# Layer 1's products with the high and low part of h side by side: 512 + 256 columns in place of three times 256

## The chip, the core and the metric

The kernel runs on one of the eight cores of one Trainium2 chip. The metric is device microseconds of one execution. Below, TensorE (PE; its weight loads are shown as PEld), VectorE (DVE), ScalarE (ACT), GpSimd (POOL) and SyncE (SP) are the engines of the core. SBUF is the working memory of 128 partitions, PSUM the accumulators into which TensorE writes. Each engine runs its own instructions in order and waits on semaphores of the others.

## The reference, cut to what matters

Two layers work on a latent stream x (256 tokens) and a context stream ctx (256 tokens), both of width 2048. Each layer makes h from a stream (RMS norm, then a scale and a shift that come from `c` or `c_ctx` through `w_mod`), multiplies it by `w_in` (2048 x 5120), sends the columns through three kinds of branches, each with its own gate, and multiplies the joined result by `w_out`:

```python
h = rmsnorm(x, g_pre[l]) * (1.0 + scale[:, None]) + shift[:, None]
proj = h @ w_in[l]                      # and proj_c = h_c @ w_in[l] for the context
a_u, a_v, a_g, b_q, b_k, b_v, b_g, c_x, c_g = split_cols(proj)
y_a = chunk_gmlp(gelu(a_u), gelu(a_v), ...) * silu(a_g)
y_b = window_attention(rope(b_q), rope(b_k), b_v, k_ctx, v_ctx, sink) * silu(b_g)
y_c = fourier_mix(c_x, w_f, b_f) * silu(c_g)
y = rmsnorm(concat(y_a, y_b, y_c) @ w_out[l], g_post[l])
x = x + gate[:, None] * y
```

In the last layer (layer 1) the context is used for keys and values only: every other column of `proj` is needed for the 256 latent tokens alone. All is float32; the kernel has to come close to that.

## The kernel before, in words

**Precise products from parts.** A float32 operand is split into a part `hi` that the fast matmul format (fp32r) holds exactly, and the rest `lo`. A product is three matmuls, hi·hi, hi·lo and lo·hi, into the same PSUM tile (`mm3`, lines 384 to 386). Weights come by DMA as 128x1024 halves of a unit into `raw`; ScalarE casts them to `whi` (L367), VectorE subtracts to get `wlo` (L368). `Stream` fetches three halves ahead; `raw` has three buffers, `whi` and `wlo` four each.

**Where h lies.** For each of the 16 k tiles of 128 features there are two SBUF tiles of 512 columns: `hh[k]` has the high part of the 256 latent tokens and then of the 256 context tokens, `hl[k]` the low parts in the same places. `make_h` fills them: VectorE multiplies (L451), ScalarE adds the shift and casts (L455), VectorE subtracts (L458).

**Units.** Most of `w_in` is worked off in units of 128 columns: `tunit` holds a 128x128 piece of the weights still in TensorE and sends h through it, 16 k tiles, three matmuls each, into one PSUM tile. In layer 0 h is 512 columns wide (both streams). In layer 1 it is 256 (latents), but for the two k units, which need both streams. a_v, v and the output projection of layer 1 are the other way around: h stands still and the weights move. Layer 1 begins with a_v and two heads of a_u, k tile by k tile (`start_av`, `start_au`), and goes on with au (2 units), cx (4), ag (4), cg (4), k (2), v, q (8), bg (8).

**Who takes a unit's product.** a_u: a gelu on ScalarE. c_x: `fourier`, with copies on ScalarE and sums on VectorE (L624), and further products. Gates: `gate`, a tanh on ScalarE (L735) and two VectorE steps (L736, L737). q and k: `rope`, four rotation copies of 32 partitions on ScalarE (L650), products with cosine and sine on VectorE (L652 to L654), then a split into hi and lo (L401, L402). All of them read the product where it lies, in PSUM.

**Attention of a head.** After the rope come the scores (`ps_sc`), the max on VectorE (L674), the exponential on ScalarE (L694), the scaling (L702), the transposition on TensorE (`ps_tp`, L722), a split of the result (L401, L402) and the products with v (`ps_o`).

**The order of the work.** TensorE's order is written out by hand: `Later` hands steps of the branches to TensorE after a given amount of product work, counted in `tick`. On the other engines a scheduler orders the instructions by priority when the kernel is built, so what is added moves other work too; the order is then fixed. VectorE also works off, behind all that, the products for layer 1's gate from `w_mod` (L245, L247), whose loads (`mraw`) share SP's queue with those of the weights. While layer 1's first units run, the context's stream is finished: its sums (`ps_rs`), its reciprocal rms as a diagonal (L412, L414 on POOL, L421) and the broadcast of that by a product (`ps_rb`, L433).

**Buffers.** Short-lived tiles share seven buffers of 2 KB per partition (`w2k`). Six PSUM banks (`mm`) serve the products, two (`ms`) the small ones.

Of the kernel before, what the change touches and what calls it, by code (L numbers as in the profile page):

```python
# [13 lines left out]
P = 128  # L14
# [13 lines left out]
def units():  # L28
    """(name, first column, columns, first k tile, k tiles): blocks of w_in of 128 x 2048 each."""
# [37 lines left out]
def trunk_kernel(ctx: ExitStack, tc: tile.TileContext, xT, xhalf, cT, wss, wsl, wmod, win, wout0, wout1, const, vec, rows,  # L67
# [24 lines left out]
    # ---- constants  # L92
# [17 lines left out]
    class low:  # L110
        """instructions that may wait for the next `n`."""
# [22 lines left out]
    # ---- modulation: columns [128, 16, stream] of scale, shift and gate  # L134
# [5 lines left out]
    def mod_cols(l, cb, ps8):  # L140
        """ps8 [128, 4, 2]: silu(c) @ w_mod for 512 columns of column block cb."""
# [12 lines left out]
    def mod_start(k0, nk):  # L154
        """scale and shift of k tiles k0 .. k0 + nk - 1 of layer 0 on the tensor engine: yields after
        each unit's products, and before the columns."""
# [39 lines left out]
    def mod_dve(l, cb, red):  # L196
        """red [128, 2, 16]: sums over the 32 partitions of each quadrant, transposed."""
# [38 lines left out]
    def mod_gate1():  # L236
        """products of silu(c) and the gate's columns of w_mod in layer 1, still to be summed over partitions."""
# [16 lines left out]
    def gate1():  # L254
        """(sum + b_mod) * g_post of layer 1's gate, on all partitions."""
# [31 lines left out]
    def pace():  # L287
        """steps of the modulation due per half of a unit, behind the latest weights on the vector engine."""
        state["owed"] += RATE.get(state["phase"], 0.0) / 2
        while state["owed"] >= 1:  # L290
            state["owed"] -= 1
            with low(LAG), tc.issue_after(W.last.ins):
                next(mods, None)

    # ---- work of other engines that hands products back to the tensor engine later
# [32 lines left out]
    # ---- weights: raw -> exact parts hi + lo, in halves of a unit, ahead of their use  # L328
# [59 lines left out]
    def part(w, c):  # L388
        """columns c of both parts; a part is a tile or a list of tiles side by side."""
# [19 lines left out]
    # ---- per-token reciprocal rms from sums over features  # L409
# [14 lines left out]
    def col_sums(ps, q, n, start=True, stop=True):  # L424
        """columns of ps: sums over the partitions of q [128, n * 128], one accumulation group."""
# [10 lines left out]
    # ---- streams in feature-major tiles  # L436
# [7 lines left out]

    def make_h(l, k, rb, streams):
        """h = x * rstd * gs + sh, as hi + lo; rb: rstd over the tokens of `streams`."""
# [6 lines left out]
        for s in streams:  # L453
            sl = slice(s * S, (s + 1) * S)
            first = A.activation(hh[k][:, sl], t[:, sl], AF.Identity, bias=sh[l][:, k, s:s + 1])  # L455
        for s in streams:
            sl = slice(s * S, (s + 1) * S)
            last = V.scalar_tensor_tensor(out=hl[k][:, sl], in0=t[:, sl], scalar=sh[l][:, k, s:s + 1],  # L458
                                          in1=hh[k][:, sl].bitcast(F32), op0=ALU.add, op1=ALU.subtract)
# [13 lines left out]
    def tunit(n, sl=None):  # L473
        """feature-major product of one unit of 128 columns: PSUM [128, n]."""
# [8 lines left out]
        return ps  # L483

# [10 lines left out]
    # ---- one layer, up to the inputs of the output projection  # L495
    def layer(l):
# [12 lines left out]
        # a_v (token-major) and two heads of a_u, k outermost  # L509
        av = [mm_ps("av") for _ in range(nt)]  # L510
        au = [mm_ps("au") for _ in range(2)]
        def start_av(k, ts):
            c = slice((k % 2) * 512, (k % 2 + 1) * 512)
            for t in ts:
                sl = slice(t * P, (t + 1) * P)
                mm3(av[t], (hh[k][:, sl], hl[k][:, sl]), part(avw, c), k == 0, k == KT - 1)

        def start_au(k):
            for j in range(2):
                c = slice((k % 4) * 256 + j * P, (k % 4) * 256 + (j + 1) * P)  # L520
                mm3(au[j][:, 0:n], part(auw, c), (hh[k][:, 0:n], hl[k][:, 0:n]), k == 0, k == KT - 1)
# [57 lines left out]
        # branch A  # L579
        def branch_a():  # L580
            vt = [w2k([P, 512]) for _ in range(nt)]
            ss = sb([P, 4], F32, "ss")
            for j in range(2):
                A.activation(ytmp(j), au[j][:, 0:n], AF.Gelu_apprx_tanh)
# [20 lines left out]
        # branch C  # L605
# [9 lines left out]
        def fourier(g, ps):  # L615
            """cos(2 pi t m / 256) is even in t around 128 and sin odd: positions t and 256 - t are added for the one
# [478 lines left out]
```

## Time and profile before

| what | value |
|---|---|
| median of 3 runs | 1171.56 us (1171.32 to 1173.29) |
| span of the profiled execution, first to last instruction | 1167.9 us (the page gives no other time of it) |
| PE busy | 1136.0 us, 97%, 6656 matmuls |
| DVE busy | 881.8 us, 76% |
| ACT busy | 509.8 us, 44% |
| layer 1: first a_v product to the start of the output projection | 759.4 to 1062.2 us |
| TensorE clock granted | 1.00 in every stage from 57 us on |

How to read it: a group of instructions has its line, engine, operation, output<-inputs, shape, count, busy time and mean duration, then the idle time of the engine just before and who ended it. Matmuls are pipelined, so their listed durations overlap and the time that one takes is read from the distance between two starts. A line of the timeline has start (us), duration (us), engine, line and operation. A line of the waits has who waited, for whom, the sum in us, the number of times and the longest. In the table of stages each pair is busy time and count of one engine.

### The profile page before, as it was taken

To read this page: it belongs to the slowest core of one execution; us is meant where nothing else is said; L and a number is where in the kernel's file an instruction comes from. 1 tells how busy PE (TensorE), PEld (TensorE's weight loads), DVE (VectorE), ACT (ScalarE), POOL (GpSimd) and SP (SyncE) were. 2 spreads that over 40 slices of the span, in tenths; PEclk is the share of its full clock that TensorE was granted. 3 is DMA by queue.
4 is the path that set the end of the run, shared out by engine and by line. 5 is a ranking of instruction groups with operands and counts; after the bars stand their busy time and mean duration, and the time that the engine had idled before them with its cause. 6 is when DMAs were issued, how large, how long until landed. Compare 5 with 4: busy or idle time off the path is not lost.

```text
span 1167.9 us, 17483 instructions
## 1 busy us (share of the span) xinstructions
PE 1136.0 (97%) x6656; PEld 953.7 (82%) x6656; DVE 881.8 (76%) x1469; ACT 509.8 (44%) x914; POOL 17.3 (1%) x23
## 2 busy tenths in 40 slices
PE   3999999999999999999999999999999999999996
PEld 1466688888898888888888888889899999997885
DVE  5454498888988878798989886495896678888554
ACT  4222513322224667632533233365563278745442
POOL 0000000000000000000000000200000000000001
PEclk9999999999999999999999999999999999999998
DMA  9999765466665334455466665365656665688563
GB/s 339 378 387 357 254 196 166 145 202 193 200 200 178 105 114 136 134 175 173 158 199 209 205 216 162 109 207 173 205 158 205 203 200 178 195 269 244 190 187 120
DMA packets 73892, 234.32 MB, mean 201 GB/s; under 512 B 8528, under 2 KB 9680, under 8 KB 73808
## 3 DMA queue, kind: packets, MB, share of 16 engines
q1 hardware_dynamic: 73808, 233.21, 61.6%
q8 instruction: 52, 0.85, 0.3%
q14 instruction: 32, 0.26, 0.1%
HBM read 231.08 MB, written 2.10 MB: 200 GB/s over the span
## 4 chain that ended last, share of the span: by engine, by line
PE 92%; DVE 3%; DMA 2%; ACT 2%; issue 1%; POOL 0%; SPq 0%; DVEq 0%; ACTq 0%; POOLq 0%
PE ps_t L384 20%; PE ps_t L385 20%; PE ps_t L386 20%; PE ps_mod L172 3%; PE ps_av L384 2%; PE ps_y L386 2%; PE ps_y L384 2%; PE ps_y L385 2%; PE ps_av L385 2%; PE ps_av L386 2%; PE ps_v L386 1%; PE ps_v L384 1%; PE ps_v L385 1%; PE ps_tp L722 1%; PE ps_au L384 1%
## 5 line engine op out<-in xcount | busy, mean ns | idle before, releaser
L384 PE MATMUL ps_t<-hh,whi 128*128 128x512 f32 (+1 forms) x1296 | 452.1, 349 | 0.0
L386 PE MATMUL ps_t<-hh,wlo 128*128 128x512 f32 (+1 forms) x1296 | 447.4, 345 | 0.0
L385 PE MATMUL ps_t<-hl,whi 128*128 128x512 f32 (+1 forms) x1296 | 447.0, 345 | 0.0
L367 ACT CAST whi<-raw 128x1024 fp32r<-128x1024 f32 x218 | 228.2, 1050 | 397.3 <-PE ps_t L385 274.4
L368 DVE TENSOR_TENSOR wlo<-raw,whi 128x1024 fp32r<-128x1024 f32 x218 | 265.3, 1220 | 99.1 <-ACT whi L367 98.8
L384 PEld LDWEIGHTS ps_t<-hh,whi 128*128 128x128 f32 x1296 | 244.9, 189 | 34.3 <-issue 4.6
L386 PEld LDWEIGHTS ps_t<-hh,wlo 128*128 128x128 f32 x1296 | 244.7, 189 | 30.6
L385 PEld LDWEIGHTS ps_t<-hl,whi 128*128 128x128 f32 x1296 | 244.9, 189 | 28.9 <-issue 0.5
L209 DVE SCALAR_TENSOR_TENSOR macc<-mraw,cs,macc 128x512 f32<-128x512 f32 x360 | 249.9, 745 | 17.6 <-DMA mraw<-in_wmod_dram 17.5
L455 ACT ACTIVATE hh<-w2k,sh 128x256 fp32r<-128x256 f32 x64 | 29.0, 502 | 61.4 <-DVE w2k L451 61.4
L384 PE MATMUL ps_y<-whi,hh 128*128 128x512 f32 x112 | 45.0, 401 | 0.0
L386 PE MATMUL ps_y<-whi,hl 128*128 128x512 f32 x112 | 43.8, 392 | 0.0
L385 PE MATMUL ps_y<-wlo,hh 128*128 128x512 f32 x112 | 43.7, 390 | 0.0
L384 PE MATMUL ps_av<-whi,hh 128*128 128x512 f32 x96 | 40.0, 416 | 0.0
L385 PE MATMUL ps_av<-wlo,hh 128*128 128x512 f32 x96 | 37.9, 395 | 0.4 <-DVE wlo L368 0.4
L172 PE MATMUL ps_mod<-hh,kt 128*32 128x512 f32 x64 | 21.5, 649 | 17.0 <-DMA hh<-in_wss_dram 17.0
L386 PE MATMUL ps_av<-whi,hl 128*128 128x512 f32 x96 | 37.6, 392 | 0.0
L386 PE MATMUL ps_v<-whi,hl 128*128 128x256 f32 x128 | 36.2, 283 | 0.0
L384 PE MATMUL ps_v<-whi,hh 128*128 128x256 f32 x128 | 36.2, 283 | 0.0
L385 PE MATMUL ps_v<-wlo,hh 128*128 128x256 f32 x128 | 36.2, 283 | 0.0
L468 DVE TENSOR_TENSOR acc<-acc,w2k 128x512 f32<-128x512 f32 (+1 forms) x33 | 21.2, 641 | 18.7 <-ACT w2k L467 17.2
L401 ACT CAST w2k<-ps_tp 128x512 fp32r<-128x512 f32 x40 | 23.5, 587 | 22.8 <-PE ps_scc L385 12.0
(292 smaller groups left out, 1491.8 us busy)
## 6 DMA issues: line engine op xcount, KB each, us to landing
raw<-in_win_dram SPq DMA_DIRECT2D x160, 512.0 KB, 4.1
mraw<-in_wmod_dram SPq DMA_DIRECT2D x128, 512.0 KB, 4.3
raw<-in_wout_dram SPq DMA_DIRECT2D x64, 512.0 KB, 4.2
hh<-in_wss_dram SPq DMA_DIRECT2D x32, 256.0 KB, 5.6
hl<-in_wss_dram SPq DMA_DIRECT2D x32, 256.0 KB, 5.4
yo<-in_xT_dram SPq DMA_DIRECT2D x16, 256.0 KB, 5.4
mraw<-in_wsl_dram SPq DMA_DIRECT2D x8, 512.0 KB, 6.9
yo<-in_wsl_dram SPq DMA_DIRECT2D x16, 256.0 KB, 7.2
```

The lines of the kernel that those rows point to most:

```text
L172: PE.matmul(ps[32 * kk:32 * kk + 32, 0:n], cpad[:, kg * 4 + kk], ws[kk], start=kg == 0, stop=kg == 3, tile_position=(0, 32 * kk))
L209: V.scalar_tensor_tensor(out=acc[:, s], in0=w[:, kk % 2], scalar=c, in1=acc[:, s], op0=ALU.mult, op1=ALU.add)
L367: A.copy(ph, r[:, c])
L368: self.last = V.tensor_tensor(out=pl, in0=r[:, c], in1=ph.bitcast(F32), op=ALU.subtract)
L384: PE.matmul(ps, st[0], mv[0], start=start, stop=False)
L385: PE.matmul(ps, st[0], mv[1], start=False, stop=False)
L386: PE.matmul(ps, st[1], mv[0], start=False, stop=stop)
L401: A.copy(hi, src)
L455: first = A.activation(hh[k][:, sl], t[:, sl], AF.Identity, bias=sh[l][:, k, s:s + 1])
L468: V.tensor_tensor(out=acc[:, sl], in0=acc[:, sl], in1=q[:, sl], op=ALU.add)
L722: PE.transpose(tp[:, (2 * j + b) * P:(2 * j + b + 1) * P], src, ident)
```

## The change

In layer 1, h is stored in another way: `hh[k]` has the latents' high part and, beside it, the latents' low part; `hl[k]` has the same of the context. A product of a unit is then two matmuls per k tile in place of three: the high part of the weights times all 512 columns (hi·hi into the left half of the PSUM tile, hi·lo into the right half), and the low part of the weights times the left 256 columns, into the left half. At the end of a unit the right half is copied to SBUF by ScalarE, and VectorE adds the left half to it (`joined`). What takes the product then reads that SBUF tile. The k units make one such pair for each stream. a_v and v still use `mm3`, with h taken from the new places, and layer 0 and both output projections are as they were. The line `ps = tunit(n)` changes in the same way in the six loops for au, cx, ag, cg, q and bg.

```diff
+    def h_of(l, k, sl):
+        if l == 0:
+            return hh[k][:, sl], hl[k][:, sl]
+        s, a = sl.start // S, sl.start % S
+        t, b = (hh, hl)[s][k], a + sl.stop - sl.start
+        return t[:, a:b], t[:, S + a:S + b]
+
     def make_h(l, k, rb, streams):
...
-            first = A.activation(hh[k][:, sl], t[:, sl], AF.Identity, bias=sh[l][:, k, s:s + 1])
+            first = A.activation(h_of(l, k, sl)[0], t[:, sl], AF.Identity, bias=sh[l][:, k, s:s + 1])
...
-            last = V.scalar_tensor_tensor(out=hl[k][:, sl], in0=t[:, sl], scalar=sh[l][:, k, s:s + 1],
-                                          in1=hh[k][:, sl].bitcast(F32), op0=ALU.add, op1=ALU.subtract)
+            hi, lo = h_of(l, k, sl)
+            last = V.scalar_tensor_tensor(out=lo, in0=t[:, sl], scalar=sh[l][:, k, s:s + 1],
+                                          in1=hi.bitcast(F32), op0=ALU.add, op1=ALU.subtract)
...
+    def mm2(ps, w, h, k):
+        PE.matmul(ps, w[0], h, start=k == 0, stop=False)
+        PE.matmul(ps[:, 0:S], w[1], h[:, 0:S], start=False, stop=k == KT - 1)
+
+    def joined(ps):
+        t = w2k([P, S])
+        A.copy(t, ps[:, S:T])
+        V.tensor_tensor(out=t, in0=t, in1=ps[:, 0:S], op=ALU.add)
+        return t
+
+    def tunit1(streams):
+        pss = [mm_ps("t") for _ in streams]
+        for k in range(KT):
+            if k % 8 == 0:
+                w = W.next()
+            for s, ps in zip(streams, pss):
+                mm2(ps, part(w, slice((k % 8) * P, (k % 8 + 1) * P)), (hh, hl)[s][k], k)
+                later.tick(PASS * S)
+        return [joined(ps) for ps in pss]
...
-                mm3(av[t], (hh[k][:, sl], hl[k][:, sl]), part(avw, c), k == 0, k == KT - 1)
+                mm3(av[t], h_of(l, k, sl), part(avw, c), k == 0, k == KT - 1)
...
-                mm3(au[j][:, 0:n], part(auw, c), (hh[k][:, 0:n], hl[k][:, 0:n]), k == 0, k == KT - 1)
+                if last:
+                    mm2(au[j], part(auw, c), hh[k], k)
+                else:
+                    mm3(au[j], part(auw, c), (hh[k], hl[k]), k == 0, k == KT - 1)
...
-                A.activation(ytmp(j), au[j][:, 0:n], AF.Gelu_apprx_tanh)
+                A.activation(ytmp(j), joined(au[j]) if last else au[j], AF.Gelu_apprx_tanh)
...
-        def rope(hi, lo, ps):
+        def rope(hi, lo, ps, ctx=None):
+            if ctx is None and hi.shape[-1] > S:
+                ctx = ps[:, S:T]
...
-                split_into(hi[:, CTX], lo[:, CTX], ps[:, S:T])
+                split_into(hi[:, CTX], lo[:, CTX], ctx)
...
 -            ps = tunit(n)
+            ps = tunit1([0])[0] if last else tunit(n)
...
-            ps = tunit(T)
+            pss = tunit1([0, 1]) if last else [tunit(T)]
...
-            rope(*kt[j], ps)
+            rope(*kt[j], *pss)
...
-                mm3(vps[t][:, 0:256], (hh[k][:, ts], hl[k][:, ts]), part(w, c), k == 0, k == KT - 1)
+                mm3(vps[t][:, 0:256], h_of(l, k, ts), part(w, c), k == 0, k == KT - 1)
```

More of the change, by code (lines that the diff above doesn't have):

```diff
@@ L743, in layer @@
         for h in (2, 3):
-            ps = tunit(n)
+            ps = tunit1([0])[0] if last else tunit(n)
             A.activation(ytmp(h), ps[:, 0:n], AF.Gelu_apprx_tanh)
@@ L748, in layer @@
         for g in range(4):
-            ps = tunit(n)
+            ps = tunit1([0])[0] if last else tunit(n)
             later.add(fourier(g, ps))
@@ L753, in layer @@
         for h in range(4):
-            ps = tunit(n)
+            ps = tunit1([0])[0] if last else tunit(n)
             gate(h, ps)
@@ L757, in layer @@
         for g in range(4):
-            ps = tunit(n)
+            ps = tunit1([0])[0] if last else tunit(n)
             gate(12 + g, ps)
@@ L782, in layer @@
         for h in range(8):
-            ps = tunit(n)
+            ps = tunit1([0])[0] if last else tunit(n)
             later.add(attention(h, ps))
@@ L787, in layer @@
         for h in range(8):
-            ps = tunit(n)
+            ps = tunit1([0])[0] if last else tunit(n)
             if h == 7:
```

## The prediction

> **What bounds the kernel now.** I read the page's busy times and chain first, then the table of busy time by stage, the releasers of TensorE, and last the order of time itself.
>
> ```profile
> span 1167.9 us, 17483 instructions
> PE 1136.0 (97%) x6656; PEld 953.7 (82%) x6656; DVE 881.8 (76%) x1469; ACT 509.8 (44%) x914; POOL 17.3 (1%) x23
> PE 92%; DVE 3%; DMA 2%; ACT 2%; issue 1%; POOL 0%; SPq 0%; DVEq 0%; ACTq 0%; POOLq 0%
> ```
>
> TensorE carries the chain: a change is worth what it takes from TensorE's stream, less the waits that it adds. Layer 1 runs from about 757 us; its stages, in the table by stage (busy us and count of each engine):
>
> ```profile
> core 0: us, PE busy (x) PEld busy (x) DVE busy (x) ACT busy (x) POOL busy (x), PEclk, DMA share, GB/s
> 797.00:855.00 58.00, 58.00 (x458) 52.58 (x457) 45.52 (x98) 31.21 (x65) 1.92 (x3) 1.00 0.56 172
> 946.00:995.00 49.00, 47.80 (x368) 45.86 (x367) 39.28 (x75) 40.18 (x82) 0.00 (x0) 1.00 0.58 184
> 995.00:1062.00 67.00, 66.31 (x543) 65.11 (x542) 60.03 (x98) 40.71 (x77) 0.00 (x0) 1.00 0.75 240
> ```
>
> VectorE is second: 80% in the first attention stretch, 90% from 995 to 1062. There the change puts work on it. TensorE's waits on other engines from 757 us on, by releaser:
>
> ```profile
> PE ps_o L385 <- DVE w2k L402: 1.7, 3, 1.0
> PE ps_x L847 <- DVE ctrh L261: 0.7, 1, 0.7
> PE ps_av L385 <- DVE wlo L368: 0.4, 1, 0.4
> PE ps_x L847 <- DVE nstrh L261: 0.4, 1, 0.4
> ```
>
> Only 3.2 us in all, so layer 1's products run end to end. Their price is the step from one start to the next; the listed 0.28 and 0.39 us overlap. In order of time, where layer 1's k products begin, where they give way to v, and where v ends:
>
> ```profile
> 891.01 0.28 PE L386 MATMUL ps_t<-hh,wlo 128*128 128x256 f32 x1
> 891.13 0.40 PE L384 MATMUL ps_t<-hh,whi 128*128 128x512 f32 x1
> 891.36 0.40 PE L385 MATMUL ps_t<-hl,whi 128*128 128x512 f32 x1
> 912.78 0.39 PE L386 MATMUL ps_t<-hh,wlo 128*128 128x512 f32 x1
> 913.01 0.28 PE L384 MATMUL ps_v<-whi,hh 128*128 128x256 f32 x1
> 936.00 0.28 PE L384 MATMUL ps_t<-hh,whi 128*128 128x256 f32 x1
> ```
>
> Between 891.13 and 913.01 lie k's 96 products of 512 columns: 21.88/96 = 227.9 ns each. Between 913.01 and 936.00 lie v's 192 of 256 columns: 22.99/192 = 119.7 ns; the last gate units, before 1062, step by 119.4. Where sizes meet (891.01 to 891.13 to 891.36) a step is set by the product that starts it, so mixing them costs nothing extra. Two of 256 take 239 ns, one of 512 takes 228: each product carries about 11 ns that its columns don't explain.
>
> **The change, part by part.**
>
> *Products.* In layer 1, 32 units (2 + 2 a_u, 4 c_x, 4 a_g, 4 c_g, 8 q, 8 b_g) have 16 k tiles each: 512 triples of 256 columns become pairs of 512 + 256. A triple costs 3 x 119.5 = 358.5 ns, a pair 227.9 + 119.5 = 347.4: 11.1 ns less, 5.7 us over 512. The two k units go the other way: 32 triples of 512 (683.7 ns) become two pairs (694.8), +0.4 us. Together 480 products fewer, the same columns, **-5.3 us**, all on the path. The two prices from different stretches put it between -5.1 and -5.5.
>
> The Trainium skill, "TensorE: Matmul & The Clock Gate", section "Back-to-back issue gap", gives an isolated step of N/2.4 + 2.5 ns, so only 2.5 ns per product beside the columns. By it the sum would be an estimated -1.2 us here; the rows above show 11 and not 2.5, and the measurement decides.
>
> *Joins.* There are 36 (one per unit, two per k unit): ScalarE copies 128x256 from PSUM, VectorE adds the other half. Nearest rows: ACT COPY yo<-ps_o L730, 128x256, 373 ns; DVE TENSOR_TENSOR w2k<-ps_t,cst L652, one input from PSUM, 421 ns. That is +13.4 us of ACT and +15.2 us of DVE, beside TensorE. Readers of the product (gelu, tanh, rotation copies, gates) then read SBUF; DVE L736 with a PSUM input takes 412 ns and L737 without 419, so their price stands. The cover: from 797 to 855 DVE is idle 12.5 us, from 946 to 995 9.7, from 995 to 1062 7.0. Without it, each join would show as 0.4 us of waiting.
>
> *One join lands in a chain.* The order of instructions on each engine shows this place. The context's rstd starts here in the timeline before:
>
> ```profile
> 808.88 0.16 DVE L412 TENSOR_SCALAR rs_a<-ps_rs 128x2 f32<-128x2 f32 x1 [1.05 <-PE ps_rs L429]
> 809.92 0.48 DVE L421 TENSOR_SCALAR w2k<-identr,rs_b 128x128 f32<-128x128 f32 x2 [0.88 <-POOL rs_b L414]
> 810.32 1.22 DVE L368 TENSOR_TENSOR wlo<-raw,whi 128x1024 fp32r<-128x1024 f32 x1
> 811.30 0.59 PE L433 MATMUL ps_rb<-w2k,ones 128*128 128x256 f32 x2
> ```
>
> Both L421 end at 810.40 and TensorE uses them at 811.30: 0.90 us of slack. After, a wlo subtraction (1.14 us start to start) and a join (0.34) stand between the two L421, and TensorE arrives 0.08 earlier (7 k tiles): 1.48 + 0.08 - 0.90 = **+0.7 us** of waiting. From below 0, if the scheduled wlo is done early; from above +1.5.
>
> *Attention.* Each q now passes copy and join before the four rotation copies (364 ns each), which before began right at the unit's end. In the timeline q's low half (DVE w2k L402) ends before ps_sc's L385 starts by 1.84, 3.56, 0.61, 2.43, 2.44, 2.56, 2.36 and 2.43 us for the eight heads. Copy, add and four copies in a row are 0.37 + 0.42 + 1.46 = 2.25 us; if all of it came on top, the waits would sum to 0.41 + 1.64 = 2.1 us. From below it is -1.7: what TensorE waits here today is the other DVE step, the low half of the transposed probabilities:
>
> ```profile
> 1008.21 0.68 DVE L402 TENSOR_TENSOR w2k<-ps_tp,w2k 128x512 fp32r<-128x512 f32 x1
> 1008.95 0.19 PEld L385 LDWEIGHTS ps_o<-w2k,vv 128*128 128x128 f32 x1 [0.34 <-DVE w2k L402]
> ```
>
> In the new order that subtraction starts 2.4 to 2.9 us behind the head's first max (the steps of what stands between), where it is 3.4 behind now (1004.85 to 1008.21), and the join comes after it. I take **+0.4 us**, near the row of today's waits; the ends are -1.7 and +6.7 (sixteen joins of 0.42 in full).
>
> *Weights, w2k buffers, queues.* From 797 to 1062 wlo is ready 3 to 15 us before its use, so 0.4 us per unit hides. One more of the seven w2k buffers is turned over per unit; today TensorE-held buffers delay ACT by under 1 us there. No DMA is added; on SP some ten neighbours mraw/raw swap, 0.33 us of issue each, under the weights' slack; POOL's order is unchanged. At 1062 wlo leads by 3.0 us and the first hl by 1.5; TensorE comes there 1.4 us earlier on the eight gate units, while DVE has 3.4 us more to do and is idle 4.5 us between 1022 and 1060: 0, with +1.5 as the upper end.
>
> *Storage of h.* The same casts and subtractions write other columns: 0.
>
> Sum: -5.3 + 0.7 + 0.4 = **-4.2 us**. The page gives the profiled execution's span, 1167.9, and no time of its own; the runs (1171.3 to 1173.3, median 1171.56) lie 3.4 to 5.4 above it, and I leave that as it is: span 1163.7, time **1167.4 us**.
>
> **Rivals.** A difference under 0.2% (2.3 us) can't be told from none.
>
> 1. *VectorE takes over from 946 to 1062 (slower).* For: 90% busy, strictly in order, and joins add 16 x 0.42 = 6.7 us. If the idle time there is all order (waits for ACT, DMA, TensorE) and none is filled, the stages grow by 6.7 and lose their own saving (16 units x 16 x 11.1 ns = 2.8): 1171.56 - 2.5 + 0.7 + 6.7 = 1176.5. It decides once over 4.1 of the 6.7 us shows as waits. Against: 16.7 us of idle DVE there, part of it waits for mraw that late work fills.
> 2. *Half of it goes back (same).* The q chain waits in full (2.1) and two of rival 1's 6.7 us remain: 1171.56 - 5.3 + 0.7 + 2.1 + 2 = 1171.1.
> 3. *A product costs its columns only (same).* If the 11 ns came from the stages and not from the count of products, the pairs would take what the triples take: nothing saved, 1.1 us of waits added, 1172.7. Against: 256 columns step by 119.4 to 119.7 in two stages, 512 by 227.9 right between them. The 2.5 ns of the Trainium skill's section named above would come near this rival, an estimated 1.2 us below it.
> 4. *Today's waits go too (faster still).* With ps_o's 1.7 us and the ps_x waits (1.1) gone and none at ps_rb: 1171.56 - 5.3 - 2.8 = 1163.5.
>
> **How the numbers follow.** Forecast 0.62, with its own range 1165.2 (no new wait and 1.1 of today's gone) to 1169.2 (1.8 us of waits more than taken, where same begins); rival 4, 0.06; rivals 2 and 3, 0.15 and 0.03; rival 1, 0.14. Faster 0.68, same 0.18, slower 0.14. The range runs from 1165.2 to 1173.9, where slower begins: it leaves out rival 4 and rival 1, 0.20.
>
> **What would show it.** Right: 6176 PE matmuls; 128x512 groups of the new helper stepping at 228 ns followed by 120; a unit of 5.56 us where one is 5.73 today; a wait of ps_rb for DVE near 809 us; ps_sc without waits over 0.5 us. Wrong: the pair at 358 ns (rival 3); waits ps_sc <- w2k or ps_o <- w2k of more than 4 us together, or DVE above 96% from 990 on (rivals 1 and 2); ps_t <- wlo or ps_y <- hl in the releasers.

## The result: slower, by 3.3 us, where faster was forecast

The changed kernel takes 1174.68 us in the median (1173.83 to 1175.62), the kernel before in the same comparison 1171.34 (1170.82 to 1173.29): the ratio is 1.0025, with a 95% interval of 1.0013 to 1.0037. The change makes the kernel a quarter of a per cent slower. The median lies 0.8 us above the upper end of the predicted range, 1173.9, and 7.3 above the forecast of 1167.4.

The page of the changed kernel, its span, the busy times and the shares of the chain that ended last:

```profile
span 1172.9 us, 16616 instructions
PE 1135.7 (97%) x6176; PEld 929.2 (79%) x6176; DVE 893.7 (76%) x1505; ACT 521.0 (44%) x950; POOL 17.5 (1%) x23
PE 88%; DVE 4%; ACT 3%; DMA 2%; issue 2%; SPq 0%; POOL 0%; DVEq 0%; ACTq 0%; POOLq 0%
```

The 480 products are gone (6656 to 6176), yet TensorE's part of the chain fell from 92 to 88%, and VectorE and ScalarE took what it lost. The same three stages of layer 1 that the prediction showed (busy us and count of each engine, granted clock, DMA share):

```profile
core 0: us, PE busy (x) PEld busy (x) DVE busy (x) ACT busy (x) POOL busy (x), PEclk, DMA share, GB/s
797.00:855.00 58.00, 54.17 (x318) 42.58 (x317) 43.99 (x99) 32.29 (x72) 2.09 (x3) 1.00 0.50 167
946.00:995.00 49.00, 48.81 (x291) 42.54 (x290) 43.69 (x82) 41.52 (x88) 0.00 (x0) 1.00 0.63 206
995.00:1062.00 67.00, 66.09 (x405) 58.26 (x404) 59.24 (x101) 44.44 (x88) 0.00 (x0) 1.00 0.68 225
```

Before, TensorE was busy for all of the 58 us from 797 to 855; now it stands still for 3.83 of them, though VectorE is no busier there than before (43.99 us against 45.52). In attention, 946 to 995, where the slower rival began, TensorE stands less than before (0.2 us for 1.2). What TensorE waits for from 700 us on, by releaser (us in total, times, longest):

```profile
PE ps_rs L981 <- ACT w2k L974: 2.4, 3, 1.4
PE ps_x L884 <- DVE ctrh L261: 2.2, 1, 2.2
PE ps_y L386 <- DVE hl L835: 1.5, 1, 1.5
PE ps_rb L433 <- DVE w2k L421: 1.1, 2, 0.6
PE ps_mix L631 <- DVE mgl L402: 0.6, 1, 0.6
PE ps_sc L384 <- ACT w2k L731: 0.6, 2, 0.4
PE ps_av L385 <- DVE wlo L368: 0.4, 1, 0.4
PE ps_o L385 <- DVE w2k L402: 0.4, 1, 0.4
```

Counted alike from 700 us on, 3.5 us of such waits became 9.2. Two groups make the difference: ps_rs, ps_rb and ps_mix between 797 and 858 us, of which the list of before has none (0.3 of ps_rs lies ahead of 757 in both), and ps_y and ps_x between 1062 and 1080, where ps_y is new and ps_x went from 1.1 to 2.2.

To add it up, I take each step from one product's start to the next, and call *gap* what it has over the usual step of its width, where that is over 0.15 us. (A small product that a stage always has costs some 0.2 us in this count, so before isn't at zero.) Gaps in us, rounded:

| stage | before | after | difference |
|---|---|---|---|
| 750-797, a_v and a_u | 1.0 | 1.2 | +0.2 |
| 797-858, a_u, branch C, the context's rstd | 2.9 | 7.7 | +4.8 |
| 858-945, gates, k, v | 0 | 0 | 0 |
| 945-1060, attention, last gates | 2.9 | 2.1 | -0.8 |
| 1060-1090, start of the last projection | 3.2 | 7.4 | +4.2 |
| all | 10.0 | 18.3 | +8.3 |

The profiled spans differ by 5.0 us (1172.9 - 1167.9), so the products themselves gave back 3.3. The runs of the changed kernel have a time 1.8 us above their span; by that the profiled execution of before took about 1169.7 and was a quick one, which is why the spans differ by more than the medians. Each gap in this document is of one execution. In 797-858 the count repeats well (2.9 in four builds without joins there), but the runs of the kernel before spread from 1169.0 to 1174.9 us over all comparisons, so a microsecond or two between two executions, in the last stage above all, needn't come from the code.

**The 797-858 us stage.** ScalarE of the changed kernel, in order of time (start us, us, engine, line, what; in brackets its idle time before and who ended it):

```profile
825.00 0.36 ACT L502 COPY w2k<-ps_t 128x256 f32<-128x256 f32 x1
...
828.74 0.48 ACT L676 ACTIVATE kt<-ps_z,vecs 128x256 f32<-128x256 f32 x1 [1.83 <-PE ps_z L386]
829.11 1.04 ACT L367 CAST whi<-raw 128x1024 fp32r<-128x1024 f32 x1
830.05 0.40 ACT L401 CAST w2k<-w2k 128x256 fp32r<-128x256 f32 x1
830.35 1.33 ACT L974 ACTIVATE w2k<-yo 128x256 f32<-128x256 f32 x4
```

and the same place before:

```profile
826.57 1.03 ACT L937 ACTIVATE w2k<-yo 128x256 f32<-128x256 f32 x3
827.99 1.05 ACT L367 CAST whi<-raw 128x1024 fp32r<-128x1024 f32 x1 [0.39 <-DMA raw<-in_win_dram]
828.94 0.46 ACT L641 ACTIVATE kt<-ps_z,vecs 128x256 f32<-128x256 f32 x1
```

Before, three squares (L937, which the rows of ps_rs need) stood ahead of the copy kt<-ps_z, and that copy waited for nothing. After, the join's copy (L502) came in, the copy kt<-ps_z stands idle 1.83 us for TensorE's ps_z, and four squares, a cast of weights and a cast of x queue up behind it in ScalarE's fixed order, while TensorE waits for the squares. The same again at 838.33 (1.28 us idle, then the squares). That is 2.1 us of the 3.8 that the list has for this stage; the rest, ps_rb's 1.1 and ps_mix's 0.6, are waits for VectorE.

The place that the prediction had named, on VectorE:

```profile
809.69 0.28 DVE L421 TENSOR_SCALAR w2k<-identr,rs_b 128x128 f32<-128x128 f32 x1 [0.88 <-POOL rs_b L414]
809.90 1.22 DVE L368 TENSOR_TENSOR wlo<-raw,whi 128x1024 fp32r<-128x1024 f32 x1
811.03 0.41 DVE L503 TENSOR_TENSOR w2k<-w2k,ps_t 128x256 f32<-128x256 f32 x1
811.36 0.28 DVE L421 TENSOR_SCALAR w2k<-identr,rs_b 128x128 f32<-128x128 f32 x1
```

**The 1062 us stage.** The last projection's first product (ps_y) starts at 1063.10. VectorE around it:

```profile
1062.33 0.75 DVE L247 SCALAR_TENSOR_TENSOR nstrl<-mraw,cs,nstrl 128x512 f32<-128x512 f32 x1
1062.99 0.42 DVE L503 TENSOR_TENSOR w2k<-w2k,ps_t 128x256 f32<-128x256 f32 x1
1063.32 1.22 DVE L368 TENSOR_TENSOR wlo<-raw,whi 128x1024 fp32r<-128x1024 f32 x1
1064.45 0.42 DVE L773 SCALAR_TENSOR_TENSOR w2k<-w2k,w2k 128x256 f32<-128x256 f32 x1
1064.79 0.42 DVE L835 TENSOR_TENSOR hl<-yo,hh 128x256 fp32r<-128x256 f32 x1
...
1073.76 0.69 DVE L261 TENSOR_TENSOR ctrh<-mraw,ps_gate 128x512 f32<-128x512 f32 x1
```

and before, where ps_y starts at 1062.22:

```profile
1057.54 0.74 DVE L247 SCALAR_TENSOR_TENSOR nstrl<-mraw,cs,nstrl 128x512 f32<-128x512 f32 x1
1058.20 2.35 DVE L368 TENSOR_TENSOR wlo<-raw,whi 128x1024 fp32r<-128x1024 f32 x2
...
1060.80 0.42 DVE L798 TENSOR_TENSOR hl<-yo,hh 128x256 fp32r<-128x256 f32 x1
...
1069.59 0.68 DVE L261 TENSOR_TENSOR ctrh<-mraw,ps_gate 128x512 f32<-128x512 f32 x1
```

The last multiply-add of the gate's modulation (L247) ends at 1063.1, where before it ended at 1058.3, 3.9 us ahead of ps_y. The first low half hl (L835) ends at 1065.2, 2.1 us behind ps_y's start instead of 1.0 ahead of it, and ctrh, which ps_x waits for, starts at 1073.76 instead of 1069.59. Then the granted clock falls for 3 us (stretches in us, PEclk is the third number from the end). Products of 512 columns step by some 430 ns in it, and the count above has that as 1.5 us of gaps:

```profile
1063.00:1075.00 12.00, 8.27 (x34) 5.60 (x33) 12.00 (x28) 8.94 (x20) 0.00 (x0) 0.99 0.63 194
1075.00:1078.00 3.00, 3.00 (x9) 2.42 (x8) 3.00 (x5) 0.59 (x1) 0.00 (x0) 0.50 0.77 244
1078.00:1090.00 12.00, 12.00 (x55) 9.18 (x55) 6.74 (x8) 4.80 (x6) 0.00 (x0) 0.99 0.78 232
```

### The profile page after: what moved, and what is told of

Same layout as the page of the kernel before. It is cut to its first block, busy times and chain, and to the rows that moved or that the text cites. A ratio compares the mean times of both kernels' runs of the same rounds, so it can differ in the third digit from the quotient of the medians.

```text
span 1172.9 us, 16616 instructions
## 1 busy us (share of the span) xinstructions
PE 1135.7 (97%) x6176; PEld 929.2 (79%) x6176; DVE 893.7 (76%) x1505; ACT 521.0 (44%) x950; POOL 17.5 (1%) x23
## 4 chain that ended last, share of the span: by engine, by line
PE 88%; DVE 4%; ACT 3%; DMA 2%; issue 2%; SPq 0%; POOL 0%; DVEq 0%; ACTq 0%; POOLq 0%
PE ps_t L384 15%; PE ps_t L386 15%; PE ps_t L385 15%; PE ps_t L496 7%; PE ps_t L497 4%; PE ps_mod L172 3%; PE ps_y L384 2%; PE ps_av L384 2%; PE ps_y L386 2%; PE ps_y L385 2%; PE ps_av L385 2%; PE ps_av L386 2%; PE ps_v L386 1%; PE ps_v L384 1%; PE ps_v L385 1%
## 5 line engine op out<-in xcount | busy, mean ns | idle before, releaser
L384 PE MATMUL ps_t<-hh,whi 128*128 128x512 f32 (+1 forms) x784 | 301.0, 384 | 0.0
L386 PE MATMUL ps_t<-hh,wlo 128*128 128x512 f32 (+1 forms) x784 | 299.4, 382 | 0.0
L385 PE MATMUL ps_t<-hl,whi 128*128 128x512 f32 (+1 forms) x784 | 299.1, 382 | 0.0
L209 DVE SCALAR_TENSOR_TENSOR macc<-mraw,cs,macc 128x512 f32<-128x512 f32 x360 | 250.1, 748 | 13.4 <-DMA mraw<-in_wmod_dram 13.2
L496 PE MATMUL ps_t<-hh,whi 128*128 128x512 f32 x512 | 186.8, 402 | 0.0
L386 PEld LDWEIGHTS ps_t<-hh,wlo 128*128 128x128 f32 x784 | 147.3, 188 | 29.3
L385 PEld LDWEIGHTS ps_t<-hl,whi 128*128 128x128 f32 x784 | 147.4, 188 | 27.3 <-issue 0.2
L497 PE MATMUL ps_t<-hh,wlo 128*128 128x256 f32 x512 | 143.4, 280 | 0.0
L463 ACT ACTIVATE hh<-w2k,sh 128x256 fp32r<-128x256 f32 x48 | 21.8, 503 | 56.4 <-DVE w2k L459 56.4
L386 PE MATMUL ps_y<-whi,hl 128*128 128x512 f32 x112 | 44.4, 397 | 1.5 <-DVE hl L835 1.5
L385 PE MATMUL ps_y<-wlo,hh 128*128 128x512 f32 x112 | 44.2, 395 | 0.0
L385 PE MATMUL ps_av<-wlo,hh 128*128 128x512 f32 x96 | 37.9, 395 | 0.4 <-DVE wlo L368 0.4
```

Of the source, the lines that this page charges most:

```text
L209: V.scalar_tensor_tensor(out=acc[:, s], in0=w[:, kk % 2], scalar=c, in1=acc[:, s], op0=ALU.mult, op1=ALU.add)
L384: PE.matmul(ps, st[0], mv[0], start=start, stop=False)
L385: PE.matmul(ps, st[0], mv[1], start=False, stop=False)
L386: PE.matmul(ps, st[1], mv[0], start=False, stop=stop)
L463: first = A.activation(h_of(l, k, sl)[0], t[:, sl], AF.Identity, bias=sh[l][:, k, s:s + 1])
L496: PE.matmul(ps, w[0], h, start=k == 0, stop=False)
```

## The experiments

Theory A: the joins' work on ScalarE and VectorE, and where it stands in their fixed orders, makes the waits. Its rivals: B, the w2k buffer that a join takes; C, TensorE merely arrives sooner. For the second place theory D names the joins of the last gates, E VectorE's own backlog, I the quicker pairs; F is about the pair's price, G and H about which engine's part of a join counts. All diffs are against the changed kernel unless said. "Lead" is how long before ps_y's start the first hl is done. The runs are named in the order in which they follow: e1 to e4, f1 with f2, f3, f4, g1 with g2, g3 with g4, and h1 to h3.

### The join's tile in a buffer of its own

```diff
-    def joined(ps):
...
-        t = w2k([P, S])
+    def joined(ps, shared=False):
...
+        t = w2k([P, S]) if shared else sb([P, S], F32, "jn")
...
-        return [joined(ps) for ps in pss]
+        return [joined(ps, len(pss) > 1) for ps in pss]
```

> The changed kernel, but the tile of a join has a buffer of its own (1 KB) instead of one of the seven shared w2k; the two joins of a k unit keep w2k. Theory A (the new waits come from the joins' work on ScalarE and VectorE and from its place in their order): the gaps stay, 1174.7 +- 0.8 us; the wait of ps_rs for the squares in 797-856 us stays above 1.5 us, since ScalarE's order in this build still has the squares of L974 behind the copies kt<-ps_z. Rival B (one user more of the seven w2k buffers makes the squares and casts late): 2.4 of ps_rs and some 2 at 1062 us go, 1170.3 +- 1.

Measured: 1181.15 us, ratio 1.0078 (1.0062 to 1.0094). In 797-858 us the gaps are 6.3 (7.7 with the shared buffers): the waits of ps_rs fell to 0.6, that of ps_rb rose to 2.2. The loss lies behind 1062, in VectorE's order:

```profile
1066.34 2.42 DVE L835 TENSOR_TENSOR hl<-yo,hh 128x256 fp32r<-128x256 f32 x7
1068.68 3.48 DVE L368 TENSOR_TENSOR wlo<-raw,whi 128x1024 fp32r<-128x1024 f32 x3
1072.09 2.31 DVE L247 SCALAR_TENSOR_TENSOR nstrl<-mraw,cs,nstrl 128x512 f32<-128x512 f32 x3
1078.58 0.69 DVE L261 TENSOR_TENSOR ctrh<-mraw,ps_gate 128x512 f32<-128x512 f32 x1 [4.17 <-DMA mraw<-in_rows_dram]
```

Three L247 now stand behind the sixteen hl and three wlo; the rows that gate1 loads into the same mraw buffers come later by as much, and ps_x waits 10.1 us for ctrh. For the first place the run decides little: A's own sign, ps_rs above 1.5, failed, and the fall of ps_rs is what B forecast, while the sum of the gaps fell by 1.4 only and the order of the squares is another here, too. That the shared buffer isn't the cause is shown further down, by the sum back in the bank and by one buffer fewer. What this run does show is that the order that the scheduler writes near 1062 can be worth 7 us by itself.

### The joins at the old number of products

```diff
-        PE.matmul(ps, w[0], h, start=k == 0, stop=False)
+        PE.matmul(ps[:, 0:S], w[0], h[:, 0:S], start=k == 0, stop=False)
+        PE.matmul(ps[:, S:T], w[0], h[:, S:T], start=False, stop=False)
```

> The joins and the side-by-side layout stay, but each pair of 512 and 256 columns becomes three products of 256 columns (hi, lo, hi parts), as many columns and as many products as before the change. Theory A (the joins cause the waits, at any pace of TensorE): no saving of 3.3 us and all or most of the 8.2 us of new gaps, 1171.3 + 5 to 8 = 1176 to 1180, forecast 1178. Rival C (TensorE arrives sooner by the faster products, and this is what opens the gaps): 1171.3 to 1173.

Measured: 1180.29 us, ratio 1.0068 (1.0052 to 1.0083). Gaps 7.1 in 797-858, 7.6 in 1060-1090: the waits are there without any quicker product, as A says, and C falls as the cause of the first group. Against this kernel the pairs are worth 5.0 us by the two ratios, 4.2 by the profiled spans. Its triples step by 119.4 ns, like those before, so the steps account for 3.3 us of it (5.8 ns in each of 576 k tiles); the rest isn't traced.

### The pairs without the joins

```diff
-        t = w2k([P, S])
-        A.copy(t, ps[:, S:T])
-        V.tensor_tensor(out=t, in0=t, in1=ps[:, 0:S], op=ALU.add)
-        return t
+        return ps[:, 0:S]
```

> The pairs of products stay, the joins are left out: consumers read the left half of the bank, so layer 1's units lack the product of w_hi with the low part of h (the right half is computed and not added). Theory A (joins cause the waits): only the saving of the products is left, 512 triples by 358.5 - 352 = 6.5 ns, 3.3 us, less some of the 3.7 us of gaps that VectorE and ScalarE already made in the second half before: 1171.3 - 3.3 = 1168.0, 1167 to 1169.5. Rival C (faster arrival makes the waits): 1171 to 1174. If the pair's price in the prediction (347.4 ns) were right: 1166.

Measured: 1168.96 us, ratio 0.9976 (0.9966 to 0.9985), 3.1 us below the runs of before beside it. Gaps 2.9 in 797-858, exactly those of before: A holds there. But behind 1060 they are 7.2, as in the changed kernel (this profile is of a run of 1170.4, one of the longer ones):

```profile
PE ps_y L386 <- DVE hl L832: 1.7, 1, 1.7
PE ps_x L881 <- DVE nstrh L261: 1.7, 1, 1.7
PE ps_x L881 <- DVE ctrh L261: 1.5, 1, 1.5
```

So that place needs no joins to go wrong in this execution; how far it goes wrong in a usual one, 1.5 us shorter, isn't shown.

### Plain triples in the last gates

```diff
-            ps = tunit1([0])[0] if last else tunit(n)
+            ps = (plain1() if h >= 0 else tunit1([0])[0]) if last else tunit(n)
             if h == 7:
```

plain1 is the unit of before on the new layout: three products of 256 columns from hh[k]'s left and right half, no join.

> The changed kernel, but the last eight gate units of layer 1 (950 to 1063 us, behind q) are triples of 256 columns without joins; all else as changed. Theory D (the joins of these units leave VectorE behind, so the first hl of L835 come late to ps_y, ctrh late to ps_x, and the clock drops behind the idle time): the 1.7, 2.55 and 1.5 us around 1063 to 1080 us shrink to the 1.8 us of the kernel before, -3.9, and 128 triples cost 6.5 ns each more, +0.8: 1174.7 - 3.1 = 1171.6, 1170.8 to 1172.6. Rival (these waits come from the sooner arrival, or from the joins of q's units): 1174.7 to 1175.6.

Measured: 1171.49 us, ratio 0.9997 (0.9987 to 1.0007). Gaps of 1060-1090 fall from 7.4 to 4.1, the wait of ps_y for hl is gone, the last L247 is done 3.7 us ahead of ps_y and the first hl leads by 0.8. The place is right and so is the time (1171.6 was forecast); whether the joins do it or the pairs, this run can't say.

### Plain triples in both places, and in the first alone

```diff
                 if last:
-                    mm2(au[j], part(auw, c), hh[k], k)
+                    mm3(au[j][:, 0:S], part(auw, c), (hh[k][:, 0:S], hh[k][:, S:T]), k == 0, k == KT - 1)
...
         for h in (2, 3):
-            ps = tunit1([0])[0] if last else tunit(n)
+            ps = plain1() if last else tunit(n)
...
         for g in range(4):
-            ps = tunit1([0])[0] if last else tunit(n)
+            ps = plain1() if last else tunit(n)
             later.add(fourier(g, ps))
```

f2 has this alone; f1 has the last gates plain as well, so that pairs and joins remain in a_g, c_g, q and k.

> Pairs and joins only in 16 gate and q units (ag, cg, q) and in k; the four a_u units, the four of branch C and the last eight gates are triples without joins. Theory A with both places: against the run with plain last gates (1171.5) the 5.0 us of new gaps in 797-858 us go, and 128 triples more cost 6.5 ns each, +0.8: 1167.4. Theory E (VectorE's own work sets when ps_y and ps_x can go on behind 1062 us, so what TensorE gains earlier is waited out there, as in the run without joins, whose gaps there were 7.2 us against 3.2): 3 us of it come back, 1170.5. The wait of ps_rs on the squares of L974 should be gone in either case.

> Only the four a_u units and the four of branch C as triples without joins; the last gates keep pairs and joins. Theory A (each place pays for itself): 1174.7 - 4.8 of gaps in 797-858 us + 0.8 = 1170.7. Theory E (the end of VectorE's work at 1062 us is fixed): TensorE comes there 4 us sooner and waits 4 us longer, 1174 to 1175, and the gaps of 1060-1090 us grow from 7.4 to about 11 us.

Measured: f1 1168.48 us, ratio 0.9976 (0.9966 to 0.9986); f2 1171.65, ratio 1.0003 (0.9994 to 1.0012). In both the gaps of 797-858 are back at 2.9. f1 lies between A's figure (1167.4) and E's (1170.5). All that f1's TensorE still waits for from 700 us on:

```profile
PE ps_x L894 <- DVE ctrh L261: 1.9, 1, 1.9
PE ps_av L385 <- DVE wlo L368: 0.4, 1, 0.4
PE ps_x L894 <- DVE nstrh L261: 0.3, 1, 0.3
PE ps_sc L384 <- ACT w2k L741: 0.3, 1, 0.3
PE ps_rs L991 <- ACT w2k L984: 0.3, 1, 0.3
PE ps_x L894 <- DVE nstrl L261: 0.2, 1, 0.2
```

f2 is 3.0 us below the changed kernel, where A said 4.0 and E nothing; its gaps behind 1060 stay at 7.7 and don't grow to 11, so VectorE's end there isn't fixed in time. f1 is the version that beats both kernels: 3.0 us below the runs of before beside it, 6.2 below the changed kernel. Its gain over before isn't the pairs' alone: by their steps they save 0.9 us there (256 times 6.1 ns, less 0.7 in k), while the gaps of 945-1060 are some 1.8 us lower than in the kernel before.

### More of the modulation in the attention units

```diff
-                k1=2.5, v1=2.5, q1=1, bg1=2.2)
+                k1=2.5, v1=2.5, q1=1.4, bg1=2.2)
```

> The changed kernel, with the steps of the gate's modulation (L247, two of 0.75 us each) due at a rate of 1.4 instead of 1 per unit in q, so that some 3 steps leave the last gate units: 4.5 us of VectorE's work done before 1000 us. Theory E: the 5.75 us of waits and slow clock behind 1062 us shrink by 3 to 4: 1171 to 1172. Rival (the joins of the last units and the order behind them hold up hl and ctrh, not the backlog): 1174 to 1175.5; or the waits move into attention (ps_sc, ps_o grow from 1.9 us): 1174 to 1177.

Measured: 1174.25 us, ratio 1.0017 (1.0006 to 1.0027). The gaps of 1060-1090 fall from 7.4 to 2.5, with every join in place: the last L247 is done 15.9 us ahead of ps_y, the first hl leads by 2.5. But attention's gaps rise from 2.1 to 5.1 (ps_sc waits 1.9 for VectorE and 0.9 for ScalarE). E's waits shrank and the rival's waits in attention came, and they nearly cancel: the moved VectorE work found no free place there.

### The product of 256 columns first in every other k tile

```diff
-        PE.matmul(ps, w[0], h, start=k == 0, stop=False)
-        PE.matmul(ps[:, 0:S], w[1], h[:, 0:S], start=False, stop=k == KT - 1)
+        if k % 2 == 0:
+            PE.matmul(ps, w[0], h, start=k == 0, stop=False)
+            PE.matmul(ps[:, 0:S], w[1], h[:, 0:S], start=False, stop=False)
+        else:
+            PE.matmul(ps[:, 0:S], w[1], h[:, 0:S], start=False, stop=False)
+            PE.matmul(ps, w[0], h, start=False, stop=k == KT - 1)
```

> The changed kernel, with the product of 256 columns first in every other k tile, so that the width changes once per pair instead of twice. Theory F (a change from 512 to 256 columns costs 5 ns and one back gains 3): the pair falls from 351 to 353 ns to 348.5, 512 pairs by 2.5 to 4 ns, 1.3 to 2 us: 1172.7 to 1173.4. Rival (a pair costs its columns and its loads in any order): the pair stays at 351 to 353 ns, 1174.7.

Measured: 1178.80 us, ratio 1.0065 (1.0048 to 1.0081), because this build's order of VectorE also puts the last three L247 behind sixteen hl and three wlo (ps_x waits 10.7 us). The pair itself did get cheaper: 349 ns in 866-940 and 348 in 1020-1060, where the changed kernel has 353 and 350. In F's size, though not in its way: the step from 512 to 512 is 232 ns and the one from 256 to 256 is 116 to 117, so in this order a product of 512 columns takes 232 ns wherever it stands, some 4 more than in k's stage before, and the strict alternation of the changed kernel takes 3 more on top (235.5 in 866-940).

### One half of a join at a time

Copy alone, and addition alone (with a table of constants in place of the copied half):

```diff
-        A.copy(t, ps[:, S:T])
-        V.tensor_tensor(out=t, in0=t, in1=ps[:, 0:S], op=ALU.add)
+        A.copy(t, ps[:, 0:S])
```

```diff
-        A.copy(t, ps[:, S:T])
-        V.tensor_tensor(out=t, in0=t, in1=ps[:, 0:S], op=ALU.add)
+        V.tensor_tensor(out=t, in0=cc("cos"), in1=ps[:, 0:S], op=ALU.add)
```

> Pairs as changed, but a join is only ScalarE's copy, of the left half; VectorE's addition is left out, and with it the product of w_hi with the low part of h in layer 1's units. Theory G (VectorE's additions and their place make the new waits of 797-858 us and of 1062 us): gaps of 797-858 us fall from 7.7 to about 3, as without joins, and the time to about 1169 to 1170. Theory H (ScalarE, where the copy stands ahead of the squares that ps_rs waits for): gaps of 797-858 us stay at 6 to 8, 1173 to 1175.

> The mirror of it: VectorE's addition as before in size (the left half plus a table that is always there), no copy on ScalarE; the same product is left out. In this build VectorE's order has two of the last multiply-adds L247 between and behind the three casts that follow the hl of L835, nearly as the run with a buffer of its own had them, where ps_x waited 10.5 us. Theory G: gaps of 797-858 us stay at 6 to 8. Theory H: they fall to about 3. In both: over 5 us of gaps at 1060-1090 us by the order of L247, 1174 to 1180.

Measured: copy alone 1170.74 us, ratio 0.9987 (0.9978 to 0.9997); addition alone 1177.28, ratio 1.0054 (1.0035 to 1.0072), with 9.4 us of ps_x <- ctrh as its order foretold. Gaps of 797-858: none 2.9, copy 4.6, addition 3.9, both 7.7. Neither G nor H: each half costs 1.0 to 1.7 us, and the two in a row, the addition behind the copy, 4.8, some 2 more than their sum. Each of the two builds leaves out the product of w_hi with the low part of h, and each has an order of its own.

### The sum back in the bank, and one shared buffer fewer

```diff
-        V.tensor_tensor(out=t, in0=t, in1=ps[:, 0:S], op=ALU.add)
-        return t
+        V.tensor_tensor(out=ps[:, 0:S], in0=t, in1=ps[:, 0:S], op=ALU.add)
+        return ps[:, 0:S]
```

and, on the kernel before:

```diff
-    W2K = 7
+    W2K = 6
```

> The changed kernel, but the sum is written back to the left half of the bank, and the consumers read it there: the w2k tile of a join is free again after the addition, some 1 us instead of 3 to 8, and no work is added or taken away. Rival B (buffers): 797-858 us loses half of its new gaps or more, 1171.5 to 1173. Theory A (work and order): ScalarE's order of squares and kt copies in this build is that of the changed kernel, so its gaps stay at 7 to 8, 1174.7 +- 0.8.

> The kernel before with six shared w2k buffers instead of seven, no joins: one buffer fewer all the time is more than a join takes. Rival B: gaps of 797-858 us rise from 2.9 to 6 or more, and the time to 1174 or more. Theory A: gaps within 1 us of the kernel before, 1171.5 to 1173.

Measured: 1177.98 us, ratio 1.0050 (1.0035 to 1.0065), and 1175.73, ratio 1.0031 (1.0020 to 1.0043). With the tile given back at once the gaps of 797-858 are 7.8; with one buffer fewer and no joins they are 3.2. B is out for this stage, though its time for the second run (1174 or more) came: six buffers cost 3.9 us in all (of 2.9 us more gaps, 1.8 are in attention), which theory A hadn't, so the buffers aren't free either; and the sum in the bank made attention worse (5.3), so g3's time missed A's figure by 3 us.

### What takes the lead at 1062

h1 is f1 with the last gates as pairs whose halves aren't added; h2 and h3 are f1 with another pace of the modulation.

```diff
-            ps = tunit1([0])[0] if last else tunit(n)
+            ps = tunit1([0], False)[0] if last else tunit(n)
             if h == 7:
```

```diff
-                k1=2.5, v1=2.5, q1=1, bg1=2.2)
+                k1=2.8, v1=2.8, q1=1, bg1=2.2)
```

```diff
-                k1=2.5, v1=2.5, q1=1, bg1=2.2)
+                k1=2.5, v1=2.5, q1=1.2, bg1=2.2)
```

> Like the run with plain a_u, branch C and last gates, but the last eight gate units are pairs whose halves are not added (they lack the product of w_hi with the low part of h). VectorE finished the gate's modulation (last L247) 4.0 us ahead of ps_y with plain gates and 0.4 us behind it with pairs and joins. Theory D (the joins, 8 additions of 0.33 us and what they push back, eat this lead): the lead stays above 2.5 us, gaps of 1060-1090 us 4 to 5.5, 1167.7 to 1169. Rival I (the quicker pairs alone eat it, as the run without any join hinted with a lead of -0.1): lead below 1 us, gaps over 6.5, 1169.5 to 1171.

> Plain a_u, branch C and last gates, and the gate's modulation due at 2.8 instead of 2.5 steps per unit in k and v, where VectorE stands idle 10.4 of 34 us: one step (two L247, 1.5 us) leaves the last gates. Theory E (the lead of the last L247 sets the waits behind 1062 us): gaps of 1060-1090 us fall from 4.8 to about 3.3, 1167 to 1168. Rival: the waits there follow hl and ctrh whatever the lead, 1168.5.

> Plain a_u, branch C and last gates, and a rate of 1.2 instead of 1 step per unit in q: one to two steps leave the last gates for the attention's units. Theory E: gaps of 1060-1090 us fall to 2.5 to 3.5; attention's gaps rise from 1.2 to 2 to 3 as at 1.4 they did to 5.1: 1167.5 to 1169.

Measured: h1 1173.05 us, ratio 1.0011 (1.0001 to 1.0020); h2 1172.17, ratio 1.0003 (0.9994 to 1.0012); h3 1173.64, ratio 1.0017 (1.0008 to 1.0025). h1's last L247 is done 0.5 us ahead of ps_y (f1: 4.0), its first hl 1.3 behind, its gaps of 1060-1090 are 9.5: pairs in the last gates lose the lead without one addition. D falls as worded: the joins there aren't needed for the waits. I holds for the lead, with a time 2 us above its range. With the joins (f2) the time is 1.4 us shorter, so they aren't even what makes it worst. In h2 and h3 the lead of L247 grew to 8.2 and 9.3 us, and yet the gaps behind 1060 rose from f1's 4.8 to 5.4 and 7.2, with 3.1 and 2.4 us more in 945-1060. h3 speaks against the lead of L247 as the measure. h2 doesn't: 1.4 us of its 5.4 are a stretch at half clock, which f1 was spared, and its waits alone fell to 4.0. All three lie 3.7 to 5.2 us above f1, after small edits, so f1's order may owe something to luck.

What does go with the gaps behind 1060 is the lead of the first hl. Over all runs whose order has no L247 behind the hl (lead, gap, in us):

| run | lead | gap | run | lead | gap |
|---|---|---|---|---|---|
| f3 | 2.5 | 2.5 | h3 | -1.3 | 7.2 |
| g4 | 1.8 | 3.6 | h1 | -1.3 | 9.5 |
| f1 | 1.1 | 4.8 | g1 | -1.8 | 6.1 |
| before | 1.0 | 3.2 | after | -2.1 | 7.4 |
| e4 | 0.8 | 4.1 | e3 | -2.3 | 7.2 |
| h2 | 0.5 | 5.4 | f2 | -2.5 | 7.7 |
| g3 | -0.6 | 6.1 | e2 | -3.2 | 7.6 |

With a lead the gaps are 2.5 to 5.4, without one 6.1 to 9.5. Two things make the table look tidier than it is: the wait of ps_y for hl is itself one of the gaps, and a stretch of 3.4 us at half clock adds some 1.4 us to after, e2, f2, g3, h2 and h3, and 6.8 us of it about twice that to h1. The gap goes with the lead; that the lead causes what is left beside these two isn't shown. e1, f4 and g2, with three L247 behind, have 13.4 to 14.7.

## Why the prediction was wrong, step by step

- **Products, -5.3.** Right in kind, too large: 3.3 us by the balance of the spans, 2.4 by the steps. The sentence that failed is that a step is set by the product that starts it, so that mixing sizes costs nothing extra. It was read off single rows that are printed to 10 ns, and what was to be seen is 3 to 8 ns. In order of time, a last gate of the changed kernel:

```profile
1049.69 0.40 PE L496 MATMUL ps_t<-hh,whi 128*128 128x512 f32 x1
1049.93 0.28 PE L497 MATMUL ps_t<-hh,wlo 128*128 128x256 f32 x1
1050.05 0.40 PE L496 MATMUL ps_t<-hh,whi 128*128 128x512 f32 x1
1050.28 0.28 PE L497 MATMUL ps_t<-hh,wlo 128*128 128x256 f32 x1
```

  The 512 steps by 230 to 240 ns and the 256 by 120; over 865-1060 us the means are 235.4 and 117.0, a pair of 352.4 instead of 347.4. Against the triple's 358.5 that leaves 6.1 ns, 3.1 us over 512, not 5.7; k's two units, at two pairs for a triple of 683.7, give back 0.7 and not 0.4. So the bounds of -5.1 and -5.5 were too narrow. The 227.9 were taken from k's stage, where all products have 512 columns, and the run with the order turned puts about 3 of the 5 ns down to the alternation; where the other 2 come from isn't shown.

- **Joins hidden under VectorE's idle time.** This is the step that turned the sign. The cover of 12.5 us in 797-855 was an average; the chain there (squares, rows of ps_rs, rstd, ps_rb) has its own due times, and what a join displaces is an order, not idle time. The stage lost 4.8 us more, against the 0.7 that the sum had for it, with 1.0 to 1.7 for either half of the joins alone, and the loss is gone in every build without joins there. The forecast looked at one place in that stage and costed it well; ScalarE's order, with the squares behind a copy that waits for TensorE, it never looked at. That the joins cause these waits is shown; that they do it by pushing the squares behind that copy is read from the order, as no run has the joins with the squares ahead of it and nothing else changed.

- **The join between the two L421, +0.7.** Right in place and mechanism; a wait of 0.6 us by the list, 0.8 as a gap.

- **Attention, +0.4.** -0.8 in this pair of executions, inside the range of -1.7 to +6.7. The reason given for the lower end held: the low half of the probabilities comes before the join in the new order, and ps_o's waits fell from 1.7 to 0.4 us, while ps_sc's rose to 0.6. (The leads that the prediction lists, 1.84 us and so on, are those to L386, the product that takes q's low half, and not to L385.) Rival 1, which put 6.7 us of waits between 946 and 1062, is refuted there, though it had the sign right and VectorE did come out of the stretch later.

- **Weights, w2k buffers, queues, 0.** The w2k part holds for 797-858 (g3, g4), and no ps_t waits for wlo. g4 shows the seventh buffer to be worth 3.9 us over the whole kernel, most of it outside that stage, so pricing one more user of the seven at nothing everywhere was more than the trace gave.

- **At 1062, 0, with +1.5 as the upper end.** Wrong: +4.2 between the two profiles, up to some 1.7 us of which may be the quick execution of before. The terms were there (TensorE sooner by 1.4, VectorE 3.4 us more to do, 4.5 idle), but the idle time was set against the work though it was idle for mraw, whose loads wait in turn for VectorE (before, from 1005 to 1063 us, SP's queue stood 9.4 us for L247 ahead of such loads); and the slow clock behind the waits, some 1.5 us in ps_y's steps, was not in the sum. The prediction's last sentence listed ps_y <- hl as a sign that it would be wrong; that is the wait that came.

- **From the profiled span to the time.** The profiled execution of before was 1.6 us quicker than its median by the 1.8 us between span and time that the later runs show. It shifts no sign, but it makes the profiles differ by 1.7 us more than the medians.

- **What stays open.** Pairs in the last gates lose the lead of hl with joins or without, and TensorE's own gain there, 8 units of 16 times 6.1 ns, 0.8 us, doesn't explain 2.4 us of lead by itself. VectorE's idle time for mraw before 1063 is 6.6 us in h1 and 4.1 in f1, and every build has its own order of VectorE there. Which of these comes first isn't shown.

## What to carry to other kernels

Work moved to an engine with idle time isn't hidden by that idle time unless it fits the order: look at each in-order engine for what the new instruction, and its producer on the other engine, will stand ahead of, above all a chain that TensorE waits for. Where a schedule is written out by a scheduler, a small edit far away can put three instructions on the wrong side of a block and cost 7 to 10 us; read the new order at the places with the least slack before the sum is made. And try such a change stage by stage: with the pairs in 16 units and k alone the kernel was 3.0 us faster than before, where all 32 units and k made it 3.3 slower. By the steps only 0.9 us of those 3.0 are the products' own; the profiles put some 1.8 down to lower gaps in attention, which came with the new order and weren't aimed at.

## What was not expected of the hardware

A product's step depends on more than its width: 512 columns step by 227.9 ns among themselves in k's stage before, by 231 to 237 in the pairs; 256 columns by 119 to 120 in triples and by 116 to 118 in pairs, even behind one another (f4). The cause isn't shown.

The granted clock fell to 0.50 for 1075 to 1078 us, behind two gaps of 1.7 and 2.4 us of TensorE some 7 us apart, and in e2 to 0.57 in 1070 to 1074 behind one of 2.8. The length of a wait doesn't decide it. In f1, with a longest wait of 1.9, the clock stayed at 1.00 from 1066 to 1074, but in f2 and h3, whose longest wait is 1.9 as well, it was 0.50 from 1062.65 to 1066.06 and from 1074.81 to 1078.22. Nor does the work done in such a time decide it by itself: in the 3.41 us ahead of the fall TensorE was busy for 1.49 in f2 and 1.55 in h3, and f1 has 3.41 us with 1.48 (1065.20 to 1068.61) and no fall. What decides isn't shown; a wait of 1.9 us can be enough, and isn't always. The Trainium skill, "TensorE: Matmul & The Clock Gate", section "What's actually happening", has the half clock after at least one idle window of about 3.4 us. No single wait in the changed kernel, e2, f2 or h3 is that long, so if an idle window means one wholly without work, the clock should have stayed there; the traces show shorter waits to be enough, and the half-rate itself as stated.
